# Convolution taps added in pairs, pooling sums on GpSimd, alpha taken out of the residual, and eight more weight tiles in three parts

## The chip, the cores and the metric

The kernel runs on one core of a Trainium2 chip. The metric is the device time of one execution in microseconds; lower is better. A core has TensorE (PE in the profile; its weight loads are PEld), VectorE (DVE), ScalarE (ACT), GpSimd (POOL) and SyncE (SP, which here issues the DMAs), each with an instruction stream of its own.

## The reference, cut to what matters

Two blocks follow each other on 256 positions of width 1024, all in float32: a retention layer with a latent-attention layer, and then a block with a convolution branch and a pooling branch. Only the second is touched:

```python
h = layer_norm(x) * (1.0 + sc1) + sh1
a_val, a_gate, u_pool, gate_a, gate_b = split(h @ w_in)        # 512, 512, 512, 1024, 1024 columns
ya = causal_dwconv(a_val * sigmoid(a_gate), w_dw_a, b_dw_a)    # 31 taps, 512 channels
ya = silu(layer_norm(ya, ln_a_g, ln_a_b)) @ w_pw_a
pooled = causal_multiscale_pool(u_pool)                        # mean over 2, 4, 8, 16 positions, less u
yb = einsum(pooled, w_pool) * pool_scale
mix = (sigmoid(gate_a) * ya + sigmoid(gate_b) * yb) @ w_out
x = layer_norm(ALPHA * x + g1 * mix, ln1_g, ln1_b)             # ALPHA = 2 ** 0.25
```

After it come a second modulation, an up projection with a three-tap convolution and a down projection.

## The kernel before

Activations lie transposed: 128 channels on the partitions, 256 positions in the columns, so a width of 1024 is eight pieces of 128x256 (`Blk`, in tiles named `half` that hold four pieces; there are 14 of them). Weights come from HBM in groups of 128x1024 (`raw`, eight tiles of 128x128) that SP loads in the order of use.

A product with a weight tile is made in one of two ways. In *three parts* (`mm`, L237 to L239) the weight group is cast by ACT to a high part (`wh`, L178), DVE subtracts that from `raw` to get the low part (`wl`, L179), the activation has been split in the same way (L187, L188), and PE runs high by high, high by low and low by high. *In float32* (`mm32`, L243) `raw` goes to PE as it is, with no work on ACT or DVE; the profile shows two matmuls for each. Both rings `wh` and `wl` have five tiles; `raw` has six, and a float32 group may lie in `wh` too. The third argument of `in_tile` chooses the way.

The second block's stage, in program order: the normalised input is modulated (`modulate`, L991 to L998) into a high part, a low part and, as `hraw`, a full copy; `k_outer` makes the last two gated tiles; then `in_tile` goes over the pooling columns (four tiles) and the two gates (sixteen tiles, in eight pairs with i from 0 to 7). Beside that DVE and ACT run the convolution of two halves of two channel pieces each (`conv_steps`), one tap of two pieces at a time: either ACT multiplies by the tap's weights into `t` and DVE adds 128x512 (L1087, L1088), or DVE multiplies and adds in two operations of 128x256 (L1091). A counter sends 53 of the 62 taps of the two halves the first way and 7 the second; the first tap of each half starts the accumulator on ACT. `pool` (L1150 on) doubles a running sum on DVE up to four times. When the convolution of a half is done, its channel sums are made on PE with a tile of ones (L1170 for the first half, L1178 for the second); `ln_a` makes the statistics, normalises, applies SiLU (L1186) and splits into `yap`, the input of `w_pw`. `fin_mix` (L1239) adds the gated product to `ax`, a copy of the input times ALPHA made at L1120.

Program order is a Python planner's: each matmul advances a clock `clk`, `after(us, fn)` queues a function by it, and `every(0.9, 62, conv)` spreads the convolution's steps. A scheduler of the language then sets each engine's final order and the waits:

```python
ax = Blk(DB)
for i in range(4):
    A.activation(ax.pair(i), xt.pair(i), AF.Copy, scale=ALPHA)
every(0.9, 62, conv)
...
in_tile(ps[:, b, :], 12 + 2 * j + b, bool(100 >> i & 1))
```

The last line gives three parts to the pairs i = 2, 5 and 6 and float32 to the other five.

Of the kernel before, what the change touches and what calls it, by code (L numbers as in the profile page):

```python
# [82 lines left out]
def tile_kernel(ctx, tc, order, xT, pT, pos, vec, cst, cv, rows, wada, wts, outT):  # L83
# [13 lines left out]
    def nm(s):  # L97
        uid[0] += 1
        return f"{s}_{uid[0]}"
# [34 lines left out]
    def t2(dt=F32):  # L134
        return tp.tile([P, 2, S], dt, tag="t2", name=nm("t2"), bufs=6)

    def t1(dt=F32, tag="t1", bufs=8):
        return tp.tile([P, S], dt, tag=tag, name=nm("t1"), bufs=bufs)
# [64 lines left out]
    def after(us, fn):  # L203
        queue.append((clk[0] + us, fn))
        queue.sort(key=lambda e: e[0])
# [72 lines left out]
    V.memset(eps_r, RMS_EPS)  # L278
    eps_l = cp.tile([P, 1], F32, name="eps_l")
    V.memset(eps_l, LN_EPS)  # L280
    A.copy(cp.tile([P, 1], F32, name="first"), eps_l)

    def col(name, i, n=1):
        o = VOFF[name] + i
        return vc[:, o:o + n]
# [79 lines left out]
    def newton(r0, ve, out, eps=None):  # L365
        t = t1()
        V.tensor_mul(t, r0, r0)
        u = t1()
        if eps is None:
            V.tensor_mul(u, ve, t)  # L370
        else:
            V.scalar_tensor_tensor(u, ve, eps, t, ADD, MUL)
        V.scalar_tensor_tensor(out, u, 3.0, r0, SUB, MUL)
        return out
# [6 lines left out]
        A.activation(r0, ps, AF.Abs_reciprocal_sqrt, bias=eps_r, scale=1.0 / n)  # L381
        return newton(r0, ve, t1(tag="nr", bufs=3) if out is None else out)

    def ln_stats(ps, n):

        mu = t1(tag="mu", bufs=2)
        A.activation(mu, ps[0], AF.Copy, scale=1.0 / n)
        msq = t1()
        A.activation(msq, ps[0], AF.Square, scale=1.0 / n)
        var = t1()  # L390
        V.scalar_tensor_tensor(var, ps[1], 1.0 / n, msq, MUL, SUB)
        r0 = t1()
        A.activation(r0, var, AF.Abs_reciprocal_sqrt, bias=eps_l)
        return mu, newton(r0, var, t1(tag="nr", bufs=3), eps=LN_EPS)

    def bc2(t, n=2):
        return t.unsqueeze(1).to_broadcast([P, n, S])
# [25 lines left out]
    def every(us, n, step):  # L423

        def run():
            step()
            if n > 1:
                every(us, n - 1, step)
        after(us, run)
# [534 lines left out]
    def mod_scales(w):  # L964
        sl = slice(8 * w, 8 * w + 8)
        V.tensor_scalar(s1[:, sl], mod[:, 8 + 24 * w:16 + 24 * w], 1.0, None, ADD)
        V.tensor_scalar(ms[:, sl], s1[:, sl], -0.5, None, MUL)
# [13 lines left out]
    def modulate(x, which, mu, nrl, pairs, pair, raw=None):  # L981

        shift = mod[:, 24 * which:24 * which + 8]
        for i in pairs:
            t = t2()
            V.tensor_sub(t, x.pair(i), bc2(mu))
            V.tensor_mul(t, t, bc2(nrl))
            for b in range(2):
                k = 2 * i + b
                m1 = ms[:, 8 * which + k:8 * which + k + 1]  # L990
                A.activation(pair[0][k], t[:, b, :], AF.Identity, bias=shift[:, k:k + 1], scale=m1)  # L991
                if raw is None:
                    full = t[:, b, :]
                    V.tensor_scalar(full, t[:, b, :], m1, shift[:, k:k + 1], MUL, ADD)
                else:
                    full = raw[k]
                    A.activation(full, t[:, b, :], AF.Identity, bias=shift[:, k:k + 1], scale=m1)
                V.tensor_sub(pair[1][k], full, pair[0][k].bitcast(F32))  # L998


# [68 lines left out]
    nc.gpsimd.memset(upt[:, :, :16], 0.0)  # L1069
    up = [upt[:, g, :] for g in range(4)]  # L1070

    acc = Blk(4)


    def conv_steps():
        n = 0
        for i0 in (0, 2):
            for k in range(31):
                w = [col("w_dw_a_2", 4 * k + i) for i in (i0, i0 + 1)]
                n += 14  # L1080
                if k == 0:
                    for b in range(2):
                        A.activation(acc[i0 + b], apad[:, i0 + b, 0:S], AF.Identity, bias=col("b_dw_a_2", i0 + b), scale=w[b])
                elif n >= 16:
                    t = t2()
                    for b in range(2):
                        A.activation(t[:, b, :], apad[:, i0 + b, k:k + S], AF.Copy, scale=w[b])  # L1087
                    V.tensor_add(acc.pair(i0 // 2), acc.pair(i0 // 2), t)  # L1088
                else:
                    for b in range(2):  # L1090
                        V.scalar_tensor_tensor(acc[i0 + b], apad[:, i0 + b, k:k + S], w[b], acc[i0 + b], MUL, ADD)  # L1091
                n %= 16
                if i0 == 2 and k == 2:
                    ln_a_first()
                if i0 == 2 and k == 30:
                    after(0.6, ln_a)
                yield

    conv_it = conv_steps()

# [14 lines left out]
    glu_ahead(0)  # L1115
    modulate(xt, 0, mu, nrl, range(2, 4), hp, hraw)
    glu_ahead(1)
    ax = Blk(DB)
    for i in range(4):
        A.activation(ax.pair(i), xt.pair(i), AF.Copy, scale=ALPHA)  # L1120
    every(0.9, 62, conv)
    pab = k_outer("w_in2", [2, 6, 3, 7], hp)
    for i in (2, 3):
        glu(pab[i - 2], i)
# [20 lines left out]
    def pool(g):  # L1145
        w = 2 << g
        s = up[g]
        for i in range(g + 1):
            n = ptile()
            V.tensor_add(n[:, 16:], s[:, 16:], s[:, 16 - (1 << i):16 + S - (1 << i)])  # L1150
            s = n
        V.scalar_tensor_tensor(pq[g][:, 16:], s[:, 32:], 1.0 / w, up[g][:, 32:], MUL, SUB)
        f = small(16)
        V.tensor_mul(f, s[:, 16:32], cc("rec", 16 * g, 16))
        V.tensor_sub(pq[g][:, 0:16], f, up[g][:, 16:32])
        split(pqp[0][g], pqp[1][g], pq[g])
# [48 lines left out]
    for i in range(8):  # L1205
        j = (i + 4) % 8
        ps = bank2()
        for b in range(2):
            in_tile(ps[:, b, :], 12 + 2 * j + b, bool(100 >> i & 1))
        A.activation(sab.pair(j), ps, AF.Sigmoid)  # L1210
        if i == 3:
            pool_out()
# [8 lines left out]

    half_outer("w_pw", yap, fin_pw, 4)

    z = Blk(DB)
    mod_scales(1)
    gs = cp.tile([P, 8], F32, name="gs")
    V.tensor_mul(gs, s1[:, 8:16], col("ln1_g_2", 0, 8))
# [8 lines left out]
    def fin_mix(ps, k0, n):  # L1236
        for b in range(n):
            k = k0 + b
            V.scalar_tensor_tensor(z[k], ps[:, b, :], mod[:, 16 + k:17 + k], ax[k], MUL, ADD)  # L1239
            A.activation(zs[k][:, :S], z[k], AF.Copy, scale=gs[:, k:k + 1])  # L1240
        if n == 2:
            sumz.feed(z.span(k0, 2))
            if k0 == 4:
                after(4.16, sumz.flush)
        else:
            if k0 == 7:
                drain()
                after(2.03, lambda: (sumz.end(z.span(7, 1), True), ln_1()))
            else:
                after(1.0, lambda: sumz.end(z.span(6, 1), False))  # L1250
# [28 lines left out]
        st["x1"] = ln_stats(sumx.ps[::-1], D)  # L1279

    def ln_1():
        st["z"] = ln_stats(sumz.ps[::-1], D)

        def part(k, n):
            if n == 2:
                sumx.feed(x1.span(k, 2))
        ln_affine(z, st["z"], 0, "ln1_b_2", x1, [1, 3, 5, 7], True, part)
        after(10.0, ln_2)
# [218 lines left out]
```

## Time and profile before

| | |
|---|---|
| runs shown | 850.41, 846.50, 850.07 us; median 850.07 |
| profiled execution | 847.85 us, its span 846.1 us |
| mean granted TensorE clock | 0.997 |
| busy share of the span: PE, PEld, DVE, ACT, POOL | 98%, 93%, 83%, 66%, 1% |

The span runs from the first to the last instruction; the execution's own time has 1.75 us around it. Timelines count from the span's start. In a row of a timeline, the first number is the start, the second how long the instruction or the run of equal instructions took; matmuls are pipelined, so the distance of two starts is what one costs, and the ends are modelled. A bracket tells how long the engine sat idle before, and what ended the wait.

### The profile page before, as it was taken

The numbers are of one execution on the slowest core, as the hardware profiler recorded it, in microseconds if no ns is written. First come the engines' busy times: TensorE is split into PE (matmuls) and PEld (weight loads), VectorE is DVE, ScalarE is ACT, GpSimd is POOL, SyncE is SP. The second block draws the span as 40 slices with busy tenths as digits, with TensorE's granted clock in tenths as the row PEclk, the third lists the DMA queues.
The fourth block names the chain that finished last, engine by engine and source line by source line (L and its number), as shares of the span: only waits on it lengthen the run. The fifth ranks groups of instructions, "written<-read, shape, count | busy, mean of one in ns | idle before, by whom it ended". The sixth has DMA issues, their size and how long they took to land.

```text
span 846.1 us, 15771 instructions
## 1 busy us (share of the span) xinstructions
PE 826.1 (98%) x6114; PEld 787.9 (93%) x6114; DVE 703.1 (83%) x1283; ACT 555.2 (66%) x968; POOL 9.9 (1%) x30
## 2 busy tenths in 40 slices
PE   8999999999999999998999999999999999999995
PEld 6989999999999989998999999999998999999885
DVE  6999798988889978688874768899677888889986
ACT  7655565545676686777754857999756576666550
POOL 0000000000000000000000000000000000000001
PEclk9999999999999999999999999999999999999998
DMA  9875567778556637374255364245463455567722
GB/s 335 323 258 212 215 217 269 255 264 319 171 182 248 223 145 259 116 263 145 99 184 176 121 224 152 98 150 199 148 224 128 134 190 191 184 214 255 277 77 75
DMA packets 46634, 167.48 MB, mean 198 GB/s; under 512 B 5216, under 2 KB 5472, under 8 KB 46560
## 3 DMA queue, kind: packets, MB, share of 16 engines
q1 hardware_dynamic: 45936, 164.38, 55.1%
q0 software_dynamic: 624, 2.10, 0.9%
q8 instruction: 48, 0.79, 0.4%
q14 instruction: 26, 0.21, 0.1%
HBM read 165.41 MB, written 1.05 MB: 197 GB/s over the span
## 4 chain that ended last, share of the span: by engine, by line
PE 50%; DVE 2%; ACT 1%; issue 1%; DVEq 0%
PE ps L238 13%; PE ps L237 13%; PE ps L239 13%; PE ps L243 10%; PE ps L341 1%; PE ps L363 0%; DVE wl L179 0%; PE ps L920 0%; PE ps L1170 0%; DVE t L1434 0%; DVE sm L1415 0%; DVE half L690 0%; DVE t L1411 0%; DVE t L1412 0%; PE ps L1407 0%
## 5 line engine op out<-in xcount | busy, mean ns | idle before, releaser
L237 PE MATMUL ps<-half,wh 128*128 128x256 f32 x1504 | 425.4, 284 | 1.4 <-ACT half L187 1.4
L238 PE MATMUL ps<-half,wh 128*128 128x256 f32 x1504 | 423.8, 282 | 0.6 <-DVE half L188 0.5
L239 PE MATMUL ps<-half,wl 128*128 128x256 f32 x1504 | 422.0, 281 | 1.1 <-DVE wl L179 1.0
L178 ACT CAST wh<-raw 128x1024 fp32r<-128x1024 f32 x233 | 243.5, 1049 | 154.9 <-PE ps L238 94.8
L179 DVE TENSOR_TENSOR wl<-raw,wh 128x1024 fp32r<-128x1024 f32 x233 | 282.7, 1219 | 59.5 <-ACT wh L178 57.3
L239 PEld LDWEIGHTS ps<-half,wl 128*128 128x128 f32 x1504 | 283.8, 189 | 1.7 <-DVE wl L179 1.7
L238 PEld LDWEIGHTS ps<-half,wh 128*128 128x128 f32 x1504 | 283.4, 188 | 1.9 <-DVE half L188 1.0
L237 PEld LDWEIGHTS ps<-half,wh 128*128 128x128 f32 x1504 | 282.5, 188 | 2.6 <-ACT half L187 2.0
L243 PE MATMUL ps<-half,raw 128*128 128x256 f32 (+2 forms) x384 | 84.9, 380 | 0.0
L243 PEld LDWEIGHTS ps<-half,raw 128*128 128x128 f32 x384 | 72.5, 190 | 10.0
L237 PE MATMUL ps<-wh,half 128*128 128x512 f32 (+1 forms) x202 | 72.6, 360 | 0.9 <-ACT wh L178 0.9
L413 DVE CUSTOM_DVE_ANT_0 adach<-adach,siluc 128x1024 f32<-128x1024 f32 x48 | 58.4, 1218 | 16.7 <-DMA adach<-in_wada 16.7
L238 PE MATMUL ps<-wl,half 128*128 128x512 f32 (+1 forms) x202 | 71.0, 351 | 0.5 <-DVE wl L179 0.5
L239 PE MATMUL ps<-wh,half 128*128 128x512 f32 (+1 forms) x202 | 71.0, 352 | 0.0
L1087 ACT ACTIVATE t<-apad,vec 128x256 f32<-128x256 f32 x106 | 44.3, 501 | 0.5 <-DVE half L1088 0.5
L237 PEld LDWEIGHTS ps<-wh,half 128*128 128x128 f32 x202 | 37.9, 188 | 6.8 <-ACT wh L178 1.7
L238 PEld LDWEIGHTS ps<-wl,half 128*128 128x128 f32 x202 | 38.1, 189 | 6.0 <-DVE wl L179 1.0
L239 PEld LDWEIGHTS ps<-wh,half 128*128 128x128 f32 x202 | 38.0, 188 | 5.6
L1088 DVE TENSOR_TENSOR half<-half,t 128x512 f32<-128x512 f32 x53 | 36.5, 689 | 3.7 <-ACT t L1087 1.8
L187 ACT CAST half<-t 128x256 fp32r<-128x256 f32 (+1 forms) x47 | 20.3, 453 | 17.9 <-DVE t L1347 10.9
L188 DVE TENSOR_TENSOR half<-t,half 128x256 fp32r<-128x256 f32 (+1 forms) x47 | 21.7, 482 | 4.5 <-ACT half L187 3.6
L1342 ACT ACTIVATE t<-ps,vec 128x256 f32<-128x256 f32 x38 | 21.0, 558 | 2.0 <-PE ps L239 1.2
(290 smaller groups left out, 908.1 us busy)
## 6 DMA issues: line engine op xcount, KB each, us to landing
raw<-in_wts SPq DMA_DIRECT2D x257, 512.0 KB, 4.1
adach<-in_wada SPq DMA_DIRECT2D x48, 512.0 KB, 5.0
half<-in_xT SPq DMA_DIRECT2D x4, 256.0 KB, 5.7
half<-in_rows POOLq DMA_DIRECT2D x2, 512.0 KB, 4.7
out<-t SPq DMA_DIRECT2D x4, 256.0 KB, 2.0
cst<-in_cst SPq DMA_DIRECT2D x1, 928.0 KB, 10.6
raw<-in_wts SPq DMA_DIRECT2D x2, 256.0 KB, 4.4
siluc<-in_cv SPq DMA_DIRECT2D x1, 512.0 KB, 9.0
```

What stands on the lines that cost most here:

```text
L178: A.copy(hi, raw)
L179: V.tensor_sub(lo, raw, hi.bitcast(F32))
L187: A.copy(hi, src)
L188: V.tensor_sub(lo, src, hi.bitcast(F32))
L237: T.matmul(ps, l[0], r[0], start=first, stop=False)
L238: T.matmul(ps, l[0], r[1], start=False, stop=False)
L239: T.matmul(ps, l[1], r[0], start=False, stop=last)
L243: T.matmul(ps, w, r, start=first, stop=last)
L413: V.tensor_tensor_reduce(ch, ch, sc, 1.0, 0.0, MUL, ADD, mod[:, n:n + 1])
L1087: A.activation(t[:, b, :], apad[:, i0 + b, k:k + S], AF.Copy, scale=w[b])
L1088: V.tensor_add(acc.pair(i0 // 2), acc.pair(i0 // 2), t)
L1342: A.activation(t[:, b, :], ps[:, b, :], AF.Identity, bias=col("b_dw_f_2", m), scale=w[2])
```

## The change

In `modulate` the full copy is made by DVE instead of ACT. The copy `ax` goes: the residual is left as x + (g1 / ALPHA) mix, with the epsilon of its normalisation divided by ALPHA squared (`eps_a`, `ga`). The convolution keeps two accumulators side by side in a tile of 128x1024 and takes two taps of two pieces at once: four products on ACT into a `half` tile, one addition of 128x1024 on DVE. A table `STEPS` says which taps DVE does alone (seven of eighteen steps for a half); at a half's end the accumulators are added. The running sums of `pool` move to GpSimd. Of the gate pairs all but i = 0 take three parts, which adds i = 1, 3, 4 and 7: eight tiles.

```diff
@@ modulate
-                if raw is None:
-                    full = t[:, b, :]
-                    V.tensor_scalar(full, t[:, b, :], m1, shift[:, k:k + 1], MUL, ADD)
-                else:
-                    full = raw[k]
-                    A.activation(full, t[:, b, :], AF.Identity, bias=shift[:, k:k + 1], scale=m1)
+                full = t[:, b, :] if raw is None else raw[k]
+                V.tensor_scalar(full, t[:, b, :], m1, shift[:, k:k + 1], MUL, ADD)
                 V.tensor_sub(pair[1][k], full, pair[0][k].bitcast(F32))
...
-    acc = Blk(4)
+    acc2 = [hp_.tile([P, 2, 2, S], F32, tag="half", name=nm("half")) for _ in range(2)]
+    def tap(i, k):
+        return apad[:, i, k:k + S], col("w_dw_a_2", 4 * k + i)
+    STEPS = [0, 0, 1, 0, 0, 1, 0, 1, 0, 1, 0, 1, 0, 1, 0, 0, 1, 0]
     def conv_steps():
...
+            for i, alone in enumerate(STEPS):
+                if alone:
+                    for b in range(2):
+                        x, w = tap(i0 + b, k)
+                        V.scalar_tensor_tensor(own[:, 0, b, :], x, w, own[:, 0, b, :], MUL, ADD)
+                else:
+                    t = hp_.tile([P, 2, 2, S], F32, tag="half", name=nm("half"))
+                    for j in range(2):
+                        for b in range(2):
+                            x, w = tap(i0 + b, k + j)
+                            A.activation(t[:, j, b, :], x, AF.Copy, scale=w)
+                    V.tensor_add(own, own, t)
+                k += 1 if alone else 2
+                if i == len(STEPS) - 1:
+                    V.tensor_add(own[:, 0], own[:, 0], own[:, 1])
...
-    ax = Blk(DB)
-    for i in range(4):
-        A.activation(ax.pair(i), xt.pair(i), AF.Copy, scale=ALPHA)
-    every(0.9, 62, conv)
+    every(1.35, 2 + 2 * len(STEPS), conv)
...
@@ pool
-            V.tensor_add(n[:, 16:], s[:, 16:], s[:, 16 - (1 << i):16 + S - (1 << i)])
+            nc.gpsimd.tensor_add(n[:, 16:], s[:, 16:], s[:, 16 - (1 << i):16 + S - (1 << i)])
...
-            in_tile(ps[:, b, :], 12 + 2 * j + b, bool(100 >> i & 1))
+            in_tile(ps[:, b, :], 12 + 2 * j + b, i > 0)
...
+    ga = cp.tile([P, 8], F32, name="ga")
+    V.tensor_scalar(ga, mod[:, 16:24], 1.0 / ALPHA, None, MUL)
...
@@ fin_mix
-            V.scalar_tensor_tensor(z[k], ps[:, b, :], mod[:, 16 + k:17 + k], ax[k], MUL, ADD)
+            V.scalar_tensor_tensor(z[k], ps[:, b, :], ga[:, k:k + 1], xt[k], MUL, ADD)
...
-        st["z"] = ln_stats(sumz.ps[::-1], D)
+        st["z"] = ln_stats(sumz.ps[::-1], D, (eps_a, LN_EPS / ALPHA ** 2))
```

The scheduler's order changes with it. First PE, where the tiles end and `w_pw` begins (`ps_7326` and `ps_7425` are the banks of the last pair of gate tiles, `ones` marks the channel sums of the convolution's second half, `half_6792`, `half_6773` and `half_6774` are `yap`). Before:

```order
L239 MATMUL ps_7246<-half_6457,wl_7286 128x256
L243 MATMUL ps_7326<-half_6454,raw_7327 128x256 x4
L1178 MATMUL ps_6936<-half_6482,ones 128x256 x2
L1178 MATMUL ps_6937<-t_1312_7337,ones 128x256 x2
L243 MATMUL ps_7326<-half_6455,raw_7327 128x256 x4
L243 MATMUL ps_7326<-half_6454,raw_7379 128x256 x4
L243 MATMUL ps_7326<-half_6455,raw_7379 128x256 x4
L237 MATMUL ps_7394<-half_6792,wh_7398 128x256
```

With the change:

```order
L239 MATMUL ps_7425<-half_6459,wl_7459 128x256
L1193 MATMUL ps_6935<-half_6485,ones 128x256 x2
L1193 MATMUL ps_6936<-t_1290_7371,ones 128x256 x2
L237 MATMUL ps_7491<-half_6773,wh_7495 128x256
L237 MATMUL ps_7492<-half_6773,wh_7495 128x256
L238 MATMUL ps_7491<-half_6774,wh_7495 128x256
L239 MATMUL ps_7491<-half_6773,wl_7496 128x256
L237 MATMUL ps_7491<-half_6773,wh_7495 128x256
```

The sums stood a quarter into the last float32 tile and had the rest of it behind them; now they stand after the last tile, and `w_pw` follows at once.

Then DVE at the end of the convolution (`half_6482` is its accumulator before, `half_6485` its second half's with the change; L1182 and L1197 begin the normalisation). Before:

```order
L1088 TENSOR_TENSOR half_6482<-half_6482,t_1307_7305 128x512
L1088 TENSOR_TENSOR half_6482<-half_6482,t_1308_7318 128x512
L179 TENSOR_TENSOR wl_7429<-raw_7426,wh_7428 128x1024
L1088 TENSOR_TENSOR half_6482<-half_6482,t_1311_7331 128x512
L179 TENSOR_TENSOR wl_7470<-raw_7467,wh_7469 128x1024
L179 TENSOR_TENSOR wl_7506<-raw_7503,wh_7505 128x1024
L1182 TENSOR_TENSOR t_1320_7357<-half_6482,t_1313_7343 128x512
L391 SCALAR_TENSOR_TENSOR t_1315_7347<-ps_6937,t_1314_7345 128x256
```

With the change:

```order
L179 TENSOR_TENSOR wl_7526<-raw_7523,wh_7525 128x1024
L1106 TENSOR_TENSOR half_6485<-half_6485,half_7358 128x1024
L179 TENSOR_TENSOR wl_7567<-raw_7564,wh_7566 128x1024
L1109 TENSOR_TENSOR half_6485<-half_6485 128x512
L179 TENSOR_TENSOR wl_7603<-raw_7600,wh_7602 128x1024
L179 TENSOR_TENSOR wl_7670<-raw_7667,wh_7669 128x1024
L1197 TENSOR_TENSOR t_1298_7391<-half_6484,t_1291_7377 128x512
L393 SCALAR_TENSOR_TENSOR t_1293_7381<-ps_6936,t_1292_7379 128x256
```

The additions are twice as wide, a low part stands behind each, and two low parts lie between the last addition (L1109) and the normalisation.

Last GpSimd, which had only the small memsets of the `lv` tiles there; with the change, in the pooling:

```order
L1165 TENSOR_TENSOR lv_6803<-upad 128x256
L1165 TENSOR_TENSOR lv_6882<-upad 128x256
L1063 MEMSET lv_6885 128x16
L1165 TENSOR_TENSOR lv_6885<-lv_6882 128x256
L1063 MEMSET lv_6996 128x16
L1063 MEMSET lv_6999 128x16
L1165 TENSOR_TENSOR lv_6996<-upad 128x256
L1165 TENSOR_TENSOR lv_6999<-lv_6996 128x256
L1063 MEMSET lv_7002 128x16
L1165 TENSOR_TENSOR lv_7002<-lv_6999 128x256
```

The ten sums stand one behind the other between those memsets; the first window has one, the last four.

## Rows read from the trace of the kernel before

**Rows 1.** The page's first part: busy time, share of the span, instructions
```profile
PE 826.1 (98%) x6114; PEld 787.9 (93%) x6114; DVE 703.1 (83%) x1283; ACT 555.2 (66%) x968; POOL 9.9 (1%) x30
```

**Rows 2.** Stretches of the second block: busy us, granted clock, DMA
```profile
core 0: us, PE busy (x) PEld busy (x) DVE busy (x) ACT busy (x) POOL busy (x), PEclk, DMA share, GB/s
550.00:560.00 10.00, 10.00 (x48) 8.81 (x47) 10.00 (x24) 9.93 (x23) 0.45 (x4) 1.00 0.30 107
```

**Rows 3.** Timeline of PE from 500: start us, us, line, operation, count
```profile
533.05 27.79 PE L243 MATMUL ps<-half,raw 128*128 128x256 f32 x128
560.48 0.47 PE L237 MATMUL ps<-half,wh 128*128 128x256 f32 x1
```

**Rows 4.** Timeline of PE from 594 to 612
```profile
593.90 0.27 PE L237 MATMUL ps<-half,wh 128*128 128x256 f32 x1
...
596.02 1.89 PE L243 MATMUL ps<-half,raw 128*128 128x256 f32 x8
597.74 1.03 PE L1178 MATMUL ps<-half,ones 128*128 128x256 f32 x4
...
599.47 5.34 PE L243 MATMUL ps<-half,raw 128*128 128x256 f32 x24
604.86 0.74 PE L237 MATMUL ps<-half,wh 128*128 128x256 f32 x4
605.44 0.29 PE L238 MATMUL ps<-half,wh 128*128 128x256 f32 x1
```

**Rows 5.** Timeline of ACT from 520 to 720
```profile
531.32 6.49 ACT L1087 ACTIVATE t<-apad,vec 128x256 f32<-128x256 f32 x16
...
599.48 1.28 ACT L393 ACT_TABLE_LOAD   x1
```

**Rows 6.** Timeline of DVE from 510 to 665
```profile
532.25 5.49 DVE L1088 TENSOR_TENSOR half<-half,t 128x512 f32<-128x512 f32 x7 [1.82 <-ACT t L1087]
537.85 0.88 DVE L1091 SCALAR_TENSOR_TENSOR half<-apad,vec,half 128x256 f32<-128x256 f32 x2
...
594.38 0.68 DVE L1088 TENSOR_TENSOR half<-half,t 128x512 f32<-128x512 f32 x1
...
599.83 0.42 DVE L391 SCALAR_TENSOR_TENSOR t<-ps,t 128x256 f32<-128x256 f32 x1
...
604.84 0.76 DVE L188 TENSOR_TENSOR half<-t,half 128x256 fp32r<-128x256 f32 x2 [0.85 <-ACT half L187]
...
621.56 3.48 DVE L179 TENSOR_TENSOR wl<-raw,wh 128x1024 fp32r<-128x1024 f32 x3
```

**Rows 7.** Groups of instructions by line: count, busy us, mean ns, idle before
```profile
L997 ACT ACTIVATE half<-t,mod,ms 128x256 f32<-128x256 f32 x8 | 4.7, 587 | 0.0
...
L1150 DVE TENSOR_TENSOR lv<-lv 128x256 f32<-128x256 f32 x6 | 2.5, 423 | 0.0
```

**Rows 8.** GpSimd's L1432, ns min/median/max, and what ran on DVE beside it
```profile
L1432 POOL TENSOR_TENSOR t<-t,half x2: 1255/1497/1739, 836.9 to 838.6; 128x512 f32<-128x512 f32 x2
...
836.85 0.69 DVE L1431 TENSOR_TENSOR t<-t,half 128x512 f32<-128x512 f32 x1
836.93 1.74 POOL L1432 TENSOR_TENSOR t<-t,half 128x512 f32<-128x512 f32 x1 [12.65 <-DVE t L1431]
...
839.66 0.78 DVE L1434 SCALAR_TENSOR_TENSOR t<-t,sm,half 128x512 f32<-128x512 f32 x1
...
840.43 0.74 DVE L1434 SCALAR_TENSOR_TENSOR t<-t,sm,half 128x512 f32<-128x512 f32 x1
```

**Rows 9.** Stretches after PE's last matmul, and two groups of matmuls
```profile
836.00:838.00 2.00, 1.36 (x12) 1.16 (x10) 1.99 (x5) 0.82 (x2) 1.07 (x1) 1.00 0.00 0
841.00:842.00 1.00, 0.00 (x0) 0.00 (x0) 0.93 (x4) 0.00 (x0) 0.00 (x0) 0.88 0.47 176
...
L276 PE MATMUL ps<-ones 128*128 128x128 f32 x18 | 4.2, 430 | 1.1 <-DVE eps_l L280 1.1
...
L1407 PE MATMUL ps<-ident,half 128*128 128x128 f32 x16 | 2.6, 272 | 0.0
```

More of the change, by code (lines that the diff above doesn't have):

```diff
@@ L280, in tile_kernel @@
     V.memset(eps_l, LN_EPS)
+    eps_a = cp.tile([P, 1], F32, name="eps_a")
+    V.memset(eps_a, LN_EPS / ALPHA ** 2)
     A.copy(cp.tile([P, 1], F32, name="first"), eps_l)
@@ L382, in rms_neg2, with ln_stats @@
         return newton(r0, ve, t1(tag="nr", bufs=3) if out is None else out)
-    def ln_stats(ps, n):
+    def ln_stats(ps, n, eps=(eps_l, LN_EPS)):
         mu = t1(tag="mu", bufs=2)
@@ L392, in ln_stats @@
         r0 = t1()
-        A.activation(r0, var, AF.Abs_reciprocal_sqrt, bias=eps_l)
-        return mu, newton(r0, var, t1(tag="nr", bufs=3), eps=LN_EPS)
+        A.activation(r0, var, AF.Abs_reciprocal_sqrt, bias=eps[0])
+        return mu, newton(r0, var, t1(tag="nr", bufs=3), eps=eps[1])
     def bc2(t, n=2):
@@ L1070, in tile_kernel, with pair @@
     up = [upt[:, g, :] for g in range(4)]
-    acc = Blk(4)
+    acc2 = [hp_.tile([P, 2, 2, S], F32, tag="half", name=nm("half")) for _ in range(2)]
+    class acc:
+        def pair(i):
+            return acc2[i][:, 0]
+    def tap(i, k):
+        return apad[:, i, k:k + S], col("w_dw_a_2", 4 * k + i)
+    STEPS = [0, 0, 1, 0, 0, 1, 0, 1, 0, 1, 0, 1, 0, 1, 0, 0, 1, 0]
     def conv_steps():
-        n = 0
         for i0 in (0, 2):
[L1078 to L1081, printed above, removed]
-                    for b in range(2):
[L1083 to L1088, printed above, removed]
-                else:
[L1090 to L1093, printed above, removed]
@@ new lines, in conv_steps @@
+            own = acc2[i0 // 2]
+            for k in range(2):
+                for b in range(2):
+                    x, w = tap(i0 + b, k)
+                    if k == 0:
+                        A.activation(own[:, k, b, :], x, AF.Identity, bias=col("b_dw_a_2", i0 + b), scale=w)
+                    else:
+                        A.activation(own[:, k, b, :], x, AF.Copy, scale=w)
+            yield
+            k = 2
+            for i, alone in enumerate(STEPS):
+                if alone:
+                    for b in range(2):
+                        x, w = tap(i0 + b, k)
+                        V.scalar_tensor_tensor(own[:, 0, b, :], x, w, own[:, 0, b, :], MUL, ADD)
+                else:
+                    t = hp_.tile([P, 2, 2, S], F32, tag="half", name=nm("half"))
[7 more added lines that the diff above has]
+                    V.tensor_add(own[:, 0], own[:, 0], own[:, 1])
+                    if i0 == 2:
+                        after(0.6, ln_a)
+                if i0 == 2 and i == 1:
@@ L1094, in conv_steps @@
                     ln_a_first()
-                if i0 == 2 and k == 30:
-                    after(0.6, ln_a)
                 yield
+            assert k == 31
     conv_it = conv_steps()
```

## Prediction

> **What bounds the kernel now.** I read the busy times first: PE 98% of the span, DVE 83%, ACT 66%, GpSimd 1% [rows 1]. The span is PE's own work; another engine counts only where PE has to wait for it. So I read the stretch in which the convolution runs: from 550 to 560 us PE, DVE and ACT are all full [rows 2]. There, a change that gives PE less and DVE more can turn the bound around. Then PE's own timeline: from 533.05 to 560.48 us 128 matmuls of L243, two for each step of a weight tile, so 64 steps in 27.43 us, 0.429 us a step [rows 3]. Near the end, eighteen three-part matmuls run from 593.90 to 596.02, six steps of 0.353 us [rows 4]. At 597.74 the channel sums of the convolution (L1178) start, at 599.47 comes the rest of the last weight tile (24 matmuls), and at 604.86 w_pw begins, whose three parts flow from 605.44 [rows 4]. These 5.4 us between the sums and w_pw are what the reader is to see: the statistics, a table load (1.28 us), SiLU and the split run meanwhile [rows 5], and the first low part starts on DVE at 604.84 [rows 6]. PE meets its input almost to the microsecond; there is no slack here.
>
> **The change, part by part.**
> *Tiles.* Eight more tiles in three parts are 64 steps, each 0.429 - 0.353 = 0.076 us shorter: PE saves 4.8 us. They cost eight casts on ACT and eight subtractions of 128x1024 on DVE, 1.14 us each by the three that took 3.48 [rows 6], so 9.1 us on DVE.
> *ACT relief.* Eight L997 (0.59) [rows 7] and the four copies of alpha x (L1120) go, and 110 tap products become 96 of 0.40 us, by sixteen in 6.49 [rows 5]: over 10 us less, against eight new casts. I take ACT at nothing, since DVE ends later. The eight L997 come back on DVE, each no longer than an addition of 256 columns (0.42) [rows 7], before the convolution, where PE still works on tiles that are there.
> *Taps.* DVE now does 22 additions of 1024 columns (the nearest shape is the 128x1024 subtraction, so 1.14), 28 single taps (0.40 each by the pair in 0.88 [rows 6]), and two of 512 columns. That is 25.1 + 11.2 + 1.2 = 37.5 us, much as before.
> *Pooling.* Ten additions of 0.42 [rows 7] leave DVE, about 3.4 us at their spacing.
> *Alpha.* One operation on eight columns is new; the residual reads xt, which lies there long before: nothing.
>
> *DVE's sum.* In the new order, between the first tap sum and the last, stand 37.5 us of taps, 18 subtractions (20.5), and about 7.5 of scalings of the pooled output (eight of 0.40), pooling rests, splits and gating: 65.5 us. The first sum starts at 532.25 now [rows 6]; it then needs eight products instead of two, but they begin about 4 us earlier, as L997 and L1120 are out of ACT's way: about 531. With about 2 us of waits (0.8 for the first GpSimd sum, the rest for products) the convolution ends at 598.5, against 594.4 + 0.7 = 595.1 now [rows 6].
> *PE's sum.* PE would be through the tiles at 604.86 - 1.73 (the sums) - 4.8 = 598.3: both arrive together.
> *The new wait.* The order of PE shows what became of the cover: the sums now stand behind the last tile and right in front of w_pw. Nothing is left to run while the statistics are made. From L1178's start to the flow of w_pw took 605.44 - 597.74 = 7.7 us [rows 4]; from 598.5 that gives 606.2. DVE also has two subtractions queued ahead of the variance, which was made at 599.83 [rows 6] and now at about 601.7; most of that hides under the table load, 0.2 us does not. So w_pw flows at 606.4 instead of 605.44: **the 4.8 us saved are given back as a wait, and 1.0 us more.** Later stages keep their order and stay PE's, so a shift here reaches the end.
>
> *GpSimd beside DVE.* No addition of 256 columns ran on GpSimd before. The two of 512 took 1.26 and 1.74 us; the longer one began at 836.93 while L1431, an addition of two SBUF tiles, was running on DVE until 837.54 [rows 8]. So an overlap cost 0.48 us. In the other direction L1434 began 0.23 us before GpSimd ended and took 0.78 instead of 0.74 [rows 8]. Nine of the ten new sums (the first runs while DVE waits for it) meet a DVE that does additions of two SBUF tiles back to back. What DVE loses is bounded below by 0.04 each, 0.4 us in all, and above by a whole 256-column sum, 1.26 / 2 = 0.63 each, 5.7 us. I take the 0.48 that the one clear overlap cost: 4.3 us. It moves the convolution's end to 602.8, behind PE, and everything after it.
> The Trainium skill's page "SBUF — State Buffer", section "Who interferes with whom", speaks against this change: a Vector instruction with two SBUF inputs and a GpSimd instruction that reads SBUF exclude each other, and the one that starts second waits for the whole of the other. By the row alone only GpSimd is seen to wait, and DVE would lose next to nothing; by the rule DVE loses too, near the upper bound. The 1.74 us row agrees with the rule in one direction; no run here shows the other yet.
>
> *Clock.* PE's last matmul ends at about 837.4, and the granted clock falls to 0.50 within the stretch 841 to 842 [rows 9]: after some 4.4 idle us. The new wait before w_pw is about 5.7 us (from 600.2 to 605.9, or the same later). At the kernel's start eighteen 128-column matmuls took 0.430 us each against 0.272 later [rows 9], so some 4.2 us ran slow before the clock rose. At half speed that would cost up to 2.1 us; nothing is the lower bound, as no row shows a fall between two stages. I take 1.0.
>
> **Sum.** -4.8 of PE work, +5.8 of wait, +4.3 for GpSimd, +1.0 for the clock: +6.3 us. The profiled execution took 847.85, so 854.2; it lies 2.2 under the median shown and 0.85 under the mean of all four executions (848.7). I forecast **855.0 us**. About 0.5%, 4.2 us, is what a measurement here tells from no change.
>
> **Rivals.**
> *GpSimd is free for DVE (0.33).* Only GpSimd waits. For it: L1434's 0.04. Against: the 0.48 lost by the other side. DVE ends at 598.5, the sum is +1.0, with a low clock up to +3.1: 849.7 to 851.8, no change that can be measured. It decides on this side as long as one overlap costs DVE less than about 0.25 us.
> *Late low parts (0.10).* DVE, full from 531 on, delivers the low parts of the new tiles one by one just in time (by the running sum the tightest is ready at 580.5 and wanted at 580.7). If the first half's sums and these tiles each make PE wait and the wh ring then holds back ACT, DVE's end slips by another 4 us: 859.
> *The saving is kept (0.07).* The sums wait for nothing and the statistics run faster on emptier engines. For a gain the gap would have to shrink from 5.4 us to under half a microsecond; the table load alone is 1.28 [rows 5]. If it did: 844.
> The forecast itself, with the clock fallen or not, has 0.50.
>
> **From these the numbers.** Slower by over 0.5%: most of the forecast (0.44), the late parts (0.10), a little of the free case with a low clock (0.03): 0.57. Same: 0.30 of the free case, 0.06 of the forecast, 0.01: 0.37. Faster: 0.06. The range, 849 to 860.5, runs from the free case without a fall of the clock to the upper bounds of GpSimd and clock on the median's side; below it lies the kept saving and a part of the free case, above it the worst late tiles.
>
> **What would show it.** Right: PE idle 5 to 6 us between the sums (now L1193) and w_pw; L243 gone from the last eight tiles; DVE full from 531 to 600; additions of 1024 columns that take 1.6 to 1.8 us instead of 1.2 while GpSimd is busy; the convolution's last addition (L1109) past 602. Wrong: GpSimd sums of about 0.7 us with DVE's durations unchanged (then the free case), a wait in front of w_pw of under 2 us (then the saving), or long PE waits for low parts in the middle of the tiles.

## The result, and the profile after

The changed kernel took 860.68 us in the median of four executions (856.09 to 861.54), the kernel before 850.24 beside it: a ratio of 1.0121, interval 1.0075 to 1.0167. Measured again with more executions (run 1 below) it was 860.13 against 851.70, a ratio of 1.0091 (1.0065 to 1.0117). So it is slower by 8 to 10 us. The profiled execution is the shortest of the four, 856.09 us with a span of 854.2, against 847.85 and 846.1 before. The forecast, 855.0, had the sign and the mechanism up to `w_pw`; the size came out larger, and the time lies 0.2 us above the range.

The page's first part, the answer to [rows 1], shows the same busy time on PE and more on DVE and GpSimd:

```profile
PE 826.4 (97%) x6178; PEld 790.3 (93%) x6178; DVE 713.1 (83%) x1276; ACT 551.4 (65%) x950; POOL 21.6 (3%) x40
```

The stretch of [rows 2], again, from the windows of the changed kernel: the three-part tiles begin earlier, DVE is still full, and GpSimd is busy for 3.7 of the 10 us.

```profile
550.00:560.00 10.00, 10.00 (x73) 9.56 (x72) 10.00 (x14) 8.61 (x19) 3.72 (x7) 1.00 0.69 238
```

PE's timeline of the changed kernel (a bracket is idle time and what ended it) answers to [rows 3, 4]:

```profile
532.83 20.88 PE L243 MATMUL ps<-half,raw 128*128 128x256 f32 x96
553.36 0.47 PE L237 MATMUL ps<-half,wh 128*128 128x256 f32 x1
...
564.46 1.13 PE L1185 MATMUL ps<-half,ones 128*128 128x256 f32 x4 [2.26 <-DVE half L1109]
...
584.82 0.39 PE L239 MATMUL ps<-half,wl 128*128 128x256 f32 x1 [1.09 <-DVE wl L179]
...
602.57 1.13 PE L1193 MATMUL ps<-half,ones 128*128 128x256 f32 x4 [0.74 <-DVE half L1109]
603.53 1.03 PE L1193 MATMUL ps<-t,ones 128*128 128x256 f32 x4
609.84 0.79 PE L237 MATMUL ps<-half,wh 128*128 128x256 f32 x2 [5.28 <-ACT half L187]
610.43 0.45 PE L238 MATMUL ps<-half,wh 128*128 128x256 f32 x1
...
844.97 0.28 PE L239 MATMUL ps<-wh,half 128*128 128x256 f32 x1
```

The first run of float32 tiles ends 7 us earlier, and no float32 gate tile comes after it now. Then PE waits four times, 9.4 us together, where it did not wait before. The longest wait stands where the order of the changed kernel had put it, between the second sums and `w_pw`. DVE's timeline shows who is late:

```profile
530.91 2.56 DVE L1106 TENSOR_TENSOR half<-half,half 128x1024 f32<-128x1024 f32 x2 [1.87 <-ACT half L1105]
...
601.83 0.68 DVE L1109 TENSOR_TENSOR half<-half 128x512 f32<-128x512 f32 x1
602.43 2.35 DVE L179 TENSOR_TENSOR wl<-raw,wh 128x1024 fp32r<-128x1024 f32 x2
...
605.30 0.42 DVE L393 SCALAR_TENSOR_TENSOR t<-ps,t 128x256 f32<-128x256 f32 x1
...
609.82 0.76 DVE L188 TENSOR_TENSOR half<-t,half 128x256 fp32r<-128x256 f32 x2 [0.85 <-ACT half L187]
```

The convolution ends at 602.51 instead of 595.06 [rows 6], and the first low part of `yap` starts at 609.82 instead of 604.84. Behind the wait the granted clock is lower (windows of the changed kernel; the column before the DMA share is the clock):

```profile
605.00:610.00 5.00, 0.16 (x1) 0.16 (x1) 4.04 (x9) 4.08 (x8) 0.00 (x0) 0.75 0.62 214
610.00:615.00 5.00, 5.00 (x26) 5.00 (x27) 1.34 (x4) 4.20 (x9) 0.00 (x0) 0.57 0.00 0
```

Both are means of stretches in which the clock is partly at the lower of its two levels, 1.2 instead of 2.4 GHz. A matmul of 256 columns takes 0.213 us there (610.68 to 610.89 in PE's timeline) instead of 0.118.

**A measure by stage.** Executions of either kernel differ by several microseconds before this stage begins, where both have the same order on PE. Run 1, the same kernel again, reached its first float32 tile at 538.35 us instead of 532.83. In the fourteen profiles of this document that start lies between 532.83 and 540.34, and the first profiles of the two kernels, 533.05 and 532.83, are the earliest. In run 1's windows the clock is low for part of the stretch near 285 us, where the other execution has 1.00:

```profile
280.00:290.00 10.00, 7.91 (x53) 7.51 (x52) 9.38 (x21) 5.67 (x10) 0.00 (x0) 0.83 0.59 192
...
570.00:575.00 5.00, 5.00 (x21) 4.35 (x22) 4.76 (x11) 4.10 (x10) 0.00 (x0) 0.66 0.00 0
```

So the runs are also compared by the **stage time**: from the start of the first matmul of the float32 tiles to the start of PE's last matmul. It is 837.08 - 533.05 = 304.0 us before, 844.97 - 532.83 = 312.1 with the change, and 311.5 in run 1. Of it, the part behind the first matmul of `w_pw` is 232.2 us before, 235.1 with the change and 234.5 in run 1; the part up to that matmul is 71.8, 77.0 and 77.0.

### The profile page after: what moved, and what is told of

The parts are those of the page before. It is cut to its first block, busy times and chain, and to the rows that moved or that the text cites. A ratio compares the mean times of both kernels' runs of the same rounds, so it can differ in the third digit from the quotient of the medians.

```text
span 854.2 us, 15883 instructions
## 1 busy us (share of the span) xinstructions
PE 826.4 (97%) x6178; PEld 790.3 (93%) x6178; DVE 713.1 (83%) x1276; ACT 551.4 (65%) x950; POOL 21.6 (3%) x40
## 4 chain that ended last, share of the span: by engine, by line
PE 43%; DVE 7%; ACT 3%; issue 1%; POOL 0%; DVEq 0%; ACTq 0%
PE ps L238 13%; PE ps L239 12%; PE ps L237 12%; PE ps L243 4%; DVE half L1106 2%; ACT half L1105 1%; DVE wl L179 1%; PE ps L343 1%; DVE half L1099 1%; POOL lv L1165 0%; PE ps L365 0%; DVE half L1218 0%; PE ps L922 0%; ACT half L993 0%; DVE t L1452 0%
## 5 line engine op out<-in xcount | busy, mean ns | idle before, releaser
L237 PE MATMUL ps<-half,wh 128*128 128x256 f32 x1568 | 443.5, 284 | 7.0 <-ACT half L187 7.0
L238 PE MATMUL ps<-half,wh 128*128 128x256 f32 x1568 | 444.3, 283 | 0.8 <-DVE half L188 0.8
L239 PE MATMUL ps<-half,wl 128*128 128x256 f32 x1568 | 440.8, 281 | 2.0 <-DVE wl L179 2.0
L178 ACT CAST wh<-raw 128x1024 fp32r<-128x1024 f32 x241 | 251.2, 1049 | 165.5 <-PE ps L238 105.0
L179 DVE TENSOR_TENSOR wl<-raw,wh 128x1024 fp32r<-128x1024 f32 x241 | 292.8, 1221 | 62.7 <-ACT wh L178 60.8
L237 PEld LDWEIGHTS ps<-half,wh 128*128 128x128 f32 x1568 | 295.6, 189 | 8.1 <-ACT half L187 7.6
L239 PEld LDWEIGHTS ps<-half,wl 128*128 128x128 f32 x1568 | 296.6, 189 | 2.6 <-DVE wl L179 2.6
L238 PEld LDWEIGHTS ps<-half,wh 128*128 128x128 f32 x1568 | 296.2, 189 | 2.3 <-DVE half L188 1.4
L243 PE MATMUL ps<-half,raw 128*128 128x260 f32 (+2 forms) x256 | 56.7, 381 | 0.0
L243 PEld LDWEIGHTS ps<-half,raw 128*128 128x128 f32 x256 | 48.4, 190 | 6.9
L1105 ACT ACTIVATE half<-apad,vec 128x256 f32<-128x256 f32 x88 | 37.2, 502 | 2.9 <-DVE half L1106 2.9
L1106 DVE TENSOR_TENSOR half<-half,half 128x1024 f32<-128x1024 f32 x22 | 27.5, 1250 | 2.5 <-ACT half L1105 1.9
```

The source lines that it names most:

```text
L178: A.copy(hi, raw)
L179: V.tensor_sub(lo, raw, hi.bitcast(F32))
L237: T.matmul(ps, l[0], r[0], start=first, stop=False)
L238: T.matmul(ps, l[0], r[1], start=False, stop=False)
L239: T.matmul(ps, l[1], r[0], start=False, stop=last)
L243: T.matmul(ps, w, r, start=first, stop=last)
```

## The experiments

All are cut from the two kernels; "DVE stretch" runs from the first product sum to the end of the convolution's last addition, by DVE's timeline, and "busy" is DVE's busy time in it, by the windows.

| run | kernel | median us, ratio to before (interval) | stage | DVE stretch, busy |
|---|---|---|---|---|
| | before | | 304.0 | 62.8, 60.8 |
| 1 | the change again | 860.13, 1.0091 (1.0065 to 1.0117) | 311.5 | 71.6, 69.2 |
| | the change, first profile | 860.68, 1.0121 (1.0075 to 1.0167) | 312.1 | 71.6, 69.2 |
| 2 | change, old tile choice | 864.23, 1.0152 (1.0127 to 1.0177) | 316.3 | 73.4, 62.3 |
| 3 | change, pooling sums on DVE | 856.36, 1.0062 (1.0035 to 1.0089) | 309.5 | 68.2, 67.6 |
| 4 | change, 20 filling matmuls | 860.28, 1.0103 (1.0082 to 1.0124) | 313.4 | |
| 5 | change, 10 filling matmuls | 857.53, 1.0068 (1.0038 to 1.0098) | 310.1 | |
| 6 | before, eight more tiles | 863.51, 1.0155 (1.0116 to 1.0193) | 316.3 | 71.8, 70.4 |
| 7 | run 2, second place for products | 853.31, 1.0024 (1.0005 to 1.0043) | 305.5 | 68.0, 61.4 |
| 8 | sums on DVE, ten tiles, second place | 858.38, 1.0082 (1.0047 to 1.0117) | 309.1 | 66.6, 63.3 |
| 9 | before, pooling sums on GpSimd | 856.10, 1.0042 (1.0016 to 1.0068) | 309.9 | 67.2, 61.8 |
| 10 | sums on DVE, eight tiles, second place | 852.37, 1.0006 (0.9984 to 1.0028) | 304.7 | 65.9, 63.1 |
| 11 | run 10, first sums later | 851.52, 1.0015 (0.9994 to 1.0036) | 304.7 | |
| 12 | change, old tiles, sums on DVE | 859.56, 1.0082 (1.0057 to 1.0108) | 311.1 | 69.4, 62.7 |

**Run 1.** No edit.

> The changed kernel as it is, once more. Theory A (DVE sets the end): the convolution's last addition ends on DVE at 602.5 us, w_pw flows 7.9 us after that, and TensorE, idle in between, comes back at half clock; what TensorE saved is worth nothing, because it only waits longer. Then the waits in front of the two channel sums (2.3 and 0.7 us) and w_pw (5.3 us) and the low clock behind them stand in any execution: a ratio of 1.010 to 1.013. Rival B (a chance state of the first executions): the ratio falls under 1.007, or the waits are other ones.

The waits came back: 2.2 us at the first sums, 0.5 at the second, 5.1 in front of `w_pw`. The ratio, 1.0091, lies just under the 1.010 that was told. Two things differ. After the 2.2 us wait that ended at 569.98 the clock fell (0.66 in the row of 570 to 575 above), while the first profile has 1.00 after its wait of 2.26. That cost nothing, because DVE was the later one: the second sums start 69.7 us after the first float32 tile in both. And the matmuls of `w_pw` ran at half pace for 2.9 us (615.36 to 618.22) instead of 4.5 (609.84 to 614.30), which is the difference of 0.6 us in the stage time.

**Run 2, the tiles taken out.**

```diff
-            in_tile(ps[:, b, :], 12 + 2 * j + b, i > 0)
+            in_tile(ps[:, b, :], 12 + 2 * j + b, bool(100 >> i & 1))
```

> The change without its eight more tiles in three parts (pairs 2, 5 and 6 alone, as before). Theory A: DVE loses eight subtractions, 9.1 us, and its convolution ends at about 593.5, before TensorE is through the tiles; TensorE is the bound again, w_pw flows within 0.5 us of 605.4, no fall of the clock, and the time is that of the kernel before within 0.2% (ratio 0.998 to 1.002). Rival B (the collisions with GpSimd or the wider additions are the loss): 4 us or more stay, a ratio of 1.005 or more.

Neither happened as told: with eight subtractions less on DVE the kernel became 4 us slower than the change. The ratio, 1.0152, is on rival B's side; the cause was another than the two that were thought of. DVE's busy time did fall, to 62.3 us, but 11 us of waiting came in. Its timeline between 572 and 583:

```profile
572.46 1.23 DVE L1106 TENSOR_TENSOR half<-half,half 128x1024 f32<-128x1024 f32 x1 [2.28 <-ACT half L1105]
575.46 1.23 DVE L1106 TENSOR_TENSOR half<-half,half 128x1024 f32<-128x1024 f32 x1 [1.77 <-ACT half L1105]
...
578.46 1.22 DVE L1106 TENSOR_TENSOR half<-half,half 128x1024 f32<-128x1024 f32 x1 [0.86 <-ACT half L1105]
...
581.46 1.22 DVE L1106 TENSOR_TENSOR half<-half,half 128x1024 f32<-128x1024 f32 x1 [0.64 <-ACT half L1105]
```

and ACT's in the same stretch:

```profile
573.73 1.70 ACT L1105 ACTIVATE half<-apad,vec 128x256 f32<-128x256 f32 x4 [0.29 <-DVE half L1106]
576.72 1.71 ACT L1105 ACTIVATE half<-apad,vec 128x256 f32<-128x256 f32 x4 [1.29 <-DVE half L1106]
```

Each waits for the other: a step of two taps takes 3.0 us, 1.7 for four products, 1.2 for the addition, and little between. So the rows look as if there were one product tile at that time. Product tiles come from the ring of fourteen `half` tiles, and by the program `hraw` keeps two of those until the last float32 tile. In the change the float32 tiles end at 553, so the ring should have room. That gave theory C, tried in run 7.

**Run 3, the pooling sums back on DVE.**

```diff
-            nc.gpsimd.tensor_add(n[:, 16:], s[:, 16:], s[:, 16 - (1 << i):16 + S - (1 << i)])
+            V.tensor_add(n[:, 16:], s[:, 16:], s[:, 16 - (1 << i):16 + S - (1 << i)])
```

> The change with the ten running sums of the pooling back on DVE. Theory A: DVE takes on 3.4 us of sums, but is rid of 3.2 us of stretched operations and of 1.6 us of waiting for GpSimd, so the convolution ends 1.3 us earlier, at about 601.2, and the kernel is 1 to 2 us faster than the change (ratio to before 1.009 to 1.011). Rival B (GpSimd relieves DVE, what it slows costs nothing): the convolution ends 3.4 us later, at about 606, and the kernel is 3 to 4 us slower than the change (ratio 1.015 or more).

Theory A's side, and by more than it said: 3.4 us off DVE's stretch, of which 1.1 is one subtraction that now stands behind the convolution's end, and 1.9 to 2.6 off the stage. How GpSimd costs DVE more than it takes over is to be read from the changed kernel's timeline of both engines:

```profile
558.94 1.21 DVE L179 TENSOR_TENSOR wl<-raw,wh 128x1024 fp32r<-128x1024 f32 x1
...
559.14 2.64 POOL L1165 TENSOR_TENSOR lv<-lv 128x256 f32<-128x256 f32 x1
560.08 1.21 DVE L1106 TENSOR_TENSOR half<-half,half 128x1024 f32<-128x1024 f32 x1
561.21 0.60 DVE L1170 TENSOR_TENSOR half<-sm,upad 128x16 f32<-128x16 f32 x1
...
561.91 0.61 POOL L1165 TENSOR_TENSOR lv<-lv 128x256 f32<-128x256 f32 x1
...
562.64 0.72 POOL L1165 TENSOR_TENSOR lv<-lv 128x256 f32<-128x256 f32 x1
563.40 0.41 DVE L1167 SCALAR_TENSOR_TENSOR half<-lv,upad 128x240 f32<-128x240 f32 x1 [1.58 <-POOL lv L1165]
563.72 0.69 DVE L1109 TENSOR_TENSOR half<-half 128x512 f32<-128x512 f32 x1
```

A sum takes GpSimd 0.61 us by itself, as at 561.91. The one at 559.14 stood through two DVE operations and ran when they were done. Then DVE's L1170, 0.17 us elsewhere, took 0.60: it stood through the sum. The page "SBUF — State Buffer" of the Trainium skill, section "Who interferes with whom", says that a DVE instruction with two SBUF inputs and a GpSimd instruction that reads SBUF exclude each other, and that the order of issue decides who waits. The trace agrees, in both directions now: GpSimd lost 2.0 us here and DVE 0.43. Late sums then make DVE wait outright, 1.58 us in front of L1167; L1109, for which PE's first sums wait, stands right behind it.

**Runs 4 and 5, PE kept at work in the wait.** After `drain()` (`la["mu"]` is the mean, kept in `ln_a` for this):

```diff
+    fill = bank()
+    for _ in range(20):      # run 5: 10
+        T.matmul(fill[:, :S], ones, la["mu"], start=True, stop=True)
```

> The change with twenty float32 matmuls of 128x256 (0.21 us each, 4.3 us in all, of the ones and the mean, their result not used) put between the second channel sums and w_pw, where TensorE waits 5.3 us. Theory A: they end before w_pw's input is there, the granted clock stays 1.00 behind the wait, and the matmuls from 609.8 to 614.2, which took 0.21 us, take 0.12: 1.9 us faster than the change (ratio to before about 1.009). Rival B (the clock falls for another reason, or its fall hides in a wait that comes later): no change against e1.

> The change with ten float32 matmuls of 128x256 between the second channel sums and w_pw instead of twenty: each of these shows as two matmuls of 0.21 us, so ten take 4.3 us, and the twenty of the last run took 8.6 and ran past the wait. Theory A (the idle wait lets the clock fall): the ten end before w_pw's input is there, the granted clock stays 1.00 behind the wait, and from the first float32 tile to TensorE's last matmul it takes 1.7 to 2 us less than the change's 311.5 to 312.1: about 310. Rival B: the clock falls all the same or something else waits there, 311.5 or more.

Run 4 was mis-sized: each of these is two matmuls in the profile, so twenty took 8.6 us and pushed `w_pw` back, to 80.2 us after the first float32 tile. Its whole time tells nothing of the clock's price; the part behind `w_pw`'s first matmul does: 233.3 us against 235.1 and 234.5. Run 5's ten fit (PE's timeline, L1232 is the filling):

```profile
607.53 1.11 PE L1193 MATMUL ps<-t,ones 128*128 128x256 f32 x4
608.48 4.48 PE L1232 MATMUL ps<-t,ones 128*128 128x256 f32 x20
613.84 0.73 PE L237 MATMUL ps<-half,wh 128*128 128x256 f32 x4 [0.88 <-ACT half L187]
```

and its windows show the full clock where the change's had 0.75 and 0.57:

```profile
605.00:610.00 5.00, 4.39 (x25) 3.64 (x24) 5.00 (x7) 3.77 (x6) 0.00 (x0) 1.00 0.82 247
610.00:615.00 5.00, 4.12 (x23) 3.44 (x22) 3.62 (x8) 4.15 (x9) 0.00 (x0) 1.00 0.46 168
```

`w_pw` starts 77.1 us after the first float32 tile, as in the change (77.0), and from there to the last matmul it takes 233.0 us. The stage took 1.4 to 2.0 us less than the change's. That is the price of the clock's fall, and the idle wait is its cause.

**Run 6, the tiles alone.** The kernel before with `i > 0` in the call of `in_tile`.

> The kernel before with the eight more tiles in three parts and nothing else of the change. Theory A (DVE sets the end): DVE gets eight subtractions, 9.1 us, of which at most 4 fall into its present waits for ScalarE, so the second channel sums start 5 to 9 us later than before's 64.7 us after the first float32 tile, and the 4.8 us that TensorE saves turn into waiting: 309 to 314 us from the first float32 tile to the last matmul against 304.0 before, a ratio of 1.006 to 1.012. Rival B (the tiles pay, the rest of the change costs): 4.8 us less, a ratio of 0.995.

The sign was right, the size too small: 12.3 us on the stage. PE's waits between 530 and 625 (in all, times, longest):

```profile
PE ps L237 <- ACT half L187: 5.6, 1, 5.6
PE ps L239 <- DVE wl L179: 4.9, 4, 3.4
```

DVE is busy for 70.4 of 71.8 us, so the subtractions had next to no gaps to go into, and the low parts themselves come late. The 12.3 us also hold the clock behind the two longest waits and a cast ahead of SiLU, of which run 12 tells.

**Run 7, theory C.** Run 2, with every other product tile in a place that is free by then:

```diff
-                    t = hp_.tile([P, 2, 2, S], F32, tag="half", name=nm("half"))
+                    turn[0] ^= 1
+                    if turn[0]:
+                        t = sp.tile([P, 2, 2, S], F32, tag="ada1", name=nm("prod"), bufs=2)
+                    else:
+                        t = hp_.tile([P, 2, 2, S], F32, tag="half", name=nm("half"))
```

> The change without its eight more tiles, as in the second run, but every other product tile of the convolution in a second place in memory (the free tile of the modulation's weights) instead of the ring of half tiles. Theory C (the ring of half tiles is the loss of the second run: the float32 copy of the input keeps two of the fourteen until the last float32 tile, ScalarE can't make the next products until DVE has added the last, and a step of two taps takes 3.0 us): steps of under 2.2 us between 570 and 585, the convolution ends 8 us or more earlier, and 304 to 309 us from the first float32 tile to the last matmul instead of 316.3; ratio 1.000 to 1.006. Rival D (GpSimd's sums or the order of the tiles hold it): 314 or more.

Theory C holds: 10.9 us less on the stage than run 2 from this edit alone (the convolution's end came 5.4 us earlier, not 8; the rest is that no cast stands ahead of SiLU now, of which run 12 tells, and that PE does not idle in front of `w_pw` and keeps its clock: 232.1 us behind `w_pw`'s first matmul against 235.1). Steps of 1.3 to 2.2 us in DVE's timeline (L1112 is the wide addition, `prod` the second place):

```profile
572.29 1.23 DVE L1112 TENSOR_TENSOR half<-half,half 128x1024 f32<-128x1024 f32 x1 [1.78 <-ACT half L1111]
573.55 1.23 DVE L1112 TENSOR_TENSOR half<-half,prod 128x1024 f32<-128x1024 f32 x1
...
575.79 1.22 DVE L1112 TENSOR_TENSOR half<-half,half 128x1024 f32<-128x1024 f32 x1
577.12 1.23 DVE L1112 TENSOR_TENSOR half<-half,prod 128x1024 f32<-128x1024 f32 x1
```

**Run 9, GpSimd alone.** The kernel before with `nc.gpsimd.tensor_add` at L1150.

> The kernel before with the ten running sums of the pooling on GpSimd and nothing else of the change. Theory A: the sums on GpSimd take 3.4 us from DVE and cost it 6.8 (the third run against the change), so its convolution ends 3.4 us later than before's 62.0 us after the first float32 tile; about 2 us of that is slack that before has at its channel sums, the rest moves w_pw: 304.5 to 306.5 us from the first float32 tile to the last matmul, a ratio of 1.001 to 1.003; DVE's operations of 0.17 us beside a sum take 0.6. Rival B (GpSimd relieves DVE): 304.0 or less, the convolution ends 2 to 3 us earlier.

More than theory A said, and by another way. The convolution did end 4.4 us later, but PE, late itself by then, did not wait there. It waited once, for a low part, because the first subtraction now came at 564.18 (558.52 before); PE's and DVE's timelines:

```profile
565.45 0.58 PE L239 MATMUL ps<-half,wl 128*128 128x256 f32 x1 [3.08 <-DVE wl L179]
...
564.18 1.22 DVE L179 TENSOR_TENSOR wl<-raw,wh 128x1024 fp32r<-128x1024 f32 x1
```

Behind that wait the matmuls start 0.213 us apart until 571.4, and the mean clock of the DVE stretch is 0.95. The wait, 3.1 us, and the slow matmuls, the other 2.8, make up the 5.9 of the stage. In how far the low part came late by the collisions or by a new order on DVE was not taken apart.

**Run 12, the taps alone** (with the small edits of `modulate` and alpha): both edits of runs 2 and 3.

> The change without its eight more tiles and with the pooling sums on DVE: what is left are the taps in pairs, the full copy on DVE and alpha out of the residual. Theory C (the ring of half tiles): in the second run DVE's 73.4 us from the first wide sum to the convolution's end held 10.8 us of waits, 1.6 of them for GpSimd; the other 9.2 stay, since the product tiles still come from that ring, so 59.1 + 9.2 = 68 us, as in the seventh run, and 305 to 308 us from the first float32 tile to the last matmul against 304.0; a ratio of 1.000 to 1.006. Rival B (GpSimd's sums were the loss of the second run, the ring costs nothing): DVE needs 59 to 60 us, TensorE is the bound, 303.5 to 304.2.

The stretch came out as said (69.4 us, with 6.8 us of waiting for products), the stage 3 us longer. ACT's timeline behind the second sums, which start at 605.76, shows why:

```profile
608.90 0.51 ACT L395 ACTIVATE t<-t,eps_l 128x256 f32<-128x256 f32 x1
611.67 1.04 ACT L178 CAST wh<-raw 128x1024 fp32r<-128x1024 f32 x1 [2.27 <-PE ps L243]
612.74 1.28 ACT L1201 ACT_TABLE_LOAD   x1
614.03 1.09 ACT L1201 ACTIVATE t<-t,vec,lng 128x256 f32<-128x256 f32 x2
```

The scheduler put a weight cast between the variance and SiLU; it waits for PE to free its tile, and the table load and SiLU wait behind it. From the sums to the first SiLU it is 8.3 us here, and 7.8 to 8.9 in runs 2, 6 and 8, against 5.7 before and 5.8 in the change. In run 3 it is 7.0, with a cast ahead of SiLU too, so run 3's stage shows less than the whole of what GpSimd cost.

**Runs 8, 10 and 11, looking for a better version:** pooling sums on DVE, the second place, and a choice of tiles between the two kernels. Run 10 also spreads the steps at 1.25, run 11 queues the first sums at 5.0.

```diff
-            in_tile(ps[:, b, :], 12 + 2 * j + b, i > 0)
+            in_tile(ps[:, b, :], 12 + 2 * j + b, i > 2)     # run 8; runs 10, 11: i in (1, 2, 5, 6)
```

> A version put together from the readings: pooling sums back on DVE, every other product tile in the second place, three parts for the pairs i = 3 to 7 (four tiles more than before instead of eight). Theory A with C: DVE's convolution takes the 68.1 us of the third run less four subtractions (4.6), so it ends 61.6 us after the first float32 tile; w_pw flows 7.9 us later, at 69.5, where TensorE, 2.4 us lighter than before, is through at 70.0; so 301.5 to 303 us to the last matmul against 304.0 before: a ratio of 0.997 to 0.999. Rival D (product tiles or casts are late while the first three pairs hold the float32 copy): 305 or more, a ratio over 1.001.

> Pooling sums on DVE, every other product tile in the second place, three parts for the pairs i = 1, 2, 5 and 6 (two tiles more than before), and the convolution's steps spread at 1.25 instead of 1.35 in the planner, so that the second channel sums stand in front of the last float32 tile, with 28 matmuls (6.0 us) behind them. Theory A with C: DVE's convolution needs 68.1 - 6 x 1.14 = 61.3 us and ends before TensorE reaches the sums; TensorE is the bound, 1.2 us lighter than before, and the statistics are covered: 302.5 to 303.5 us from the first float32 tile to the last matmul against 304.0, a ratio of 0.996 to 0.999. Rival D (late products or casts between statistics and w_pw): 304.5 or more.

> The tenth run's kernel with the first channel sums queued 5.0 instead of 2.0 us after the convolution's first half in the planner, which moves them behind seven steps of the next tile; there TensorE waited 1.3 us for DVE. Theory A: that wait goes, nothing else changes, 303.2 to 303.6 us from the first float32 tile to the last matmul (before 304.0, the tenth run 304.7), a ratio of 0.996 to 1.000. Rival D: the wait comes back at the second sums or at w_pw, 304.5 or more.

All three missed. Run 8's convolution ended 64.7 us after the first float32 tile instead of 61.6, with 3.3 us of gaps, and a cast held SiLU as in run 12. Run 10 met its order but PE waited 1.3 us for the first sums, more than the 1.2 it had been spared; in run 11 the first of those sums kept its place, and the wait stayed at 1.2. No version here was measured faster than the kernel before; the nearest is run 10, 1.0006 (0.9984 to 1.0028).

## Why the prediction was right or wrong

- **Up to `w_pw`: right.** `w_pw` was to flow, that is to run on its three parts, at 610.7 (606.4 + 4.3), and flowed at 610.43. The two sums together with `w_pw` cost PE 0.74 and 5.28 us of idling where 5.8 was told, and earlier PE waited 2.26 and 1.09 us, which with the 0.2 over 5.8 is most of GpSimd's 4.3. The saved time turned into waiting; run 6 shows that the eight tiles alone do this. One reading was wrong and harmless: the 24 matmuls that covered the statistics before are one and a half float32 tiles, not the rest of the last one.
- **DVE's sum: right to 0.3 us.** The convolution was to end at 602.8 and ended at 602.51.
- **GpSimd beside DVE: the mechanism and about the size.** 4.3 us and 0.8 of waiting were told. By the starts in DVE's timelines the change's stretch less run 3's is 3.40 us; add the 3.36 that the ten sums take on DVE in run 3, take off 1.13 of the subtraction ordered later and 0.22 of three small operations, and 5.4 us are left. The form differed: not every wide addition was stretched. Eight operations lost 0.3 to 0.43 each, and 1.6 us went into one wait for late sums. Additions of 1.6 to 1.8 us, as told, were the exception: 22 have a median of 1.217.
- **Clock: the step that failed.** Its mechanism was right and its size was not. It was taken at 1.0 between 0 and 2.1; run 5 gives 1.4 to 2.0. `w_pw`'s matmuls ran at half pace for 4.5 us in the first profile and 2.9 in run 1, where the prediction had taken the middle of its bounds. Behind `w_pw`'s first matmul the change lost 2.9 us, and 2.3 in run 1, where 1.0 was told; run 5 leaves 0.8 of it.
- **Pace: not foreseen.** These 0.8 us are another loss. The prediction had it that later stages keep their order, "so a shift here reaches the end", and nothing more. From the 1300th matmul before the last, where the order is the same in all kernels, it took PE 181.2 us instead of 180.4, spread evenly over some 1000 of them, in the first profile and in runs 1, 4 and 5 alike. It took 181.6 in run 6, 180.7 in run 3, and 180.2 to 180.4 in all other runs. The runs over 180.4 are those with all eight more tiles; why is open.
- **The base: the other step that failed.** The sum was set on 848.7, the mean of the executions shown, and its rows on a profile that reached the stage early. The executions beside the change have a median of 850.24, further ones of the kernel before medians of 850.2 to 852.7. The change's stage costs 7.5 to 8.1 us, and 8.4 over the 851.7 of run 1 is the time measured. The forecast's +6.3 is short by 1.2 to 1.8 us in clock and pace; the rest of the 5.7 us between 855.0 and 860.68 is the base and the scatter of the executions. The range did not come out of its own terms either: the upper bounds of GpSimd and clock give +8.8, and 850.07 + 8.8 is 858.9, not 860.5.
- **Rivals.** GpSimd free for DVE fell with runs 3 and 9, where DVE's convolution ended later with the sums on GpSimd. Late low parts forecast 859, nearer to the measured time than the forecast, but not by what happened: a low part was late once (1.09 us at 584.82), and DVE's end did not slip. The saving was not kept.
- **What the prediction did not see** and did not need for the sum: why the change is no worse. Its parts alone cost the stage 12.3 us (tiles, run 6), 5.9 (GpSimd, run 9) and 7.1 (taps, run 12), and all together 7.5 to 8.1. In part these count the same thing more than once: each of the three runs has its own falls of the clock, and runs 6 and 12 a cast ahead of SiLU. Beyond that, the taps in pairs want product tiles, and the extra three-part tiles free `hraw`, and with it two of them, early. This is argued from the program and from run 7; no run freed `hraw`'s tiles and nothing else. If it holds, costing ACT at nothing was safe only because of it.

## What to carry to other kernels

Where two engines meet to the microsecond, a step that moves work from one to the other is priced by the engine that ends last, and the moved work comes back as idle time of the first, with a clock loss on top. A wider intermediate is also a demand on a ring of buffers: ask which long-lived tile holds the ring's places at that time. Parts of one change need not add up, so take out one at a time before judging any of them.

## What the runs showed of the hardware that was not expected

A wait of some 2.2 us in front of the first sums was followed by a fall of the clock in run 1 and by none in the first profile, in the same kernel. A GpSimd addition of 256 columns took 0.61 us at its shortest and 2.64 where two DVE operations ran beside it, and DVE's smallest operations (16 columns) paid as much for a meeting, 0.43 us, as its widest.
